# Norm factors and row sums through DRAM on GpSimd's queue, a doubled sample column in the second norm, and low parts on 128 columns

## The chip, the cores and the metric

The kernel runs on one core of a Trainium2 chip. Such a core has five engines with instruction streams of their own: TensorE (PE in the profile; its weight loads are listed apart as PEld) multiplies matrices, VectorE (DVE) and ScalarE (ACT) work elementwise and reduce along rows, GpSimd (POOL) does the same more slowly, and SyncE (SP) issues nearly all transfers (DMAs) between DRAM and the on-chip memory. Engines wait for each other and for transfers through semaphores. Metric: device time of one execution in microseconds; less is better.

## The reference

One inference step of a two-layer decoder on 256 prompt tokens and 64 sample tokens (8 sequences of 8), all in float32, with 1024 model columns. Layer A is a spatial-gating MLP, layer B an mLSTM; each is followed by a gated MLP with a short convolution. What the change touches:

```python
def rmsnorm(x, g):
    y = x * rsqrt(mean(x * x, axis=-1) + EPS)       # one factor per token
    return y * g

def chunk_spatial_gating(x, w_in, ln_g, ln_b, w_s, b_s, w_out):   # layer A, x already rmsnormed
    h = gelu(x @ w_in)
    u, v = split(h, 2, axis=-1)                      # 2048 columns each
    v = layernorm(v) * ln_g + ln_b
    ws = where(tril, w_s, 0)                         # 8 groups of 128 x 128
    mixed = einsum('gts,bnsgd->bntgd', ws, v) + b_s  # tokens mixed in chunks of 128
    return (u * mixed) @ w_out, v
```

Two vectors matter here. The norm factor of a token scales everything that is computed from it. The row sum of ws (over s, for each group g and token t) is needed because ln_b, the same for all tokens, goes through the mixing as ln_b times the row sum.

## The kernel before

Activations are kept transposed: 1024 model columns as 8 blocks k of 128 partitions, the 320 tokens along the free axis (256 prompt, then 64 sample). Weights come from DRAM as float32 chunks `raw` of 128 x 1024 on SP's queue, several ahead. Each chunk is split for TensorE into a high part `wh` (a cast to the rounded type fp32r, on ScalarE, line 180) and a low part `wl = raw - wh` (VectorE, line 181). Activations are split in the same way into xh and xl. A product is three matmuls: xh by wh, xl by wh, xh by wl. All matmuls are issued through one helper, line 49.

The norm factor isn't applied to the activations before the product but to its result. Squares of x are summed over blocks into `acc` (128 x 320). `norm_cols` turns it into factors by token on partitions (`rc`, 128 x 3: two groups of 128 prompt tokens and one of tokens 192 to 319, of which the last 64 are the samples): three matmuls by a matrix of ones into `pc`, a scale on VectorE, a power on GpSimd. `norm_row` needs the same factors along the free axis, on all partitions (`rb`, 128 x 320): it splits rc, multiplies it into an identity (`dg`), and two matmuls `pb` with ones as the stationary side spread the diagonals over all partitions; ScalarE copies them to `rb`.

Layer A (`layer_a`) first computes v with tokens on partitions. The 2048 columns of v are done in four groups q of 512, each over the 8 blocks k; for each k the two prompt groups take three matmuls each into `pv`, and the sample group two into `pvs`: the stationary side xs holds the 64 sample columns of xh on its left and those of xl on its right, and gives high times wh and low times wh at once on 128 partitions; the product of the high samples by wl needs only the left 64 columns, and uses only those. Results of group q are taken (gelu) while the next group runs. Between the groups stand small steps:

- after four blocks of q=1, norm_cols;
- after q=1, `load_ws`: loads of the mixing matrix `ws_a` (512 KB), a block copy `wss_a` for the samples, masks `trit` and `bdt`, the bias `bs_a` and the gate weights `wg`, and their masking on GpSimd;
- after q=2, `norm_row` and `row_sums`, which splits ws_a into high and low parts and adds its rows by four matmuls with ones (`pr`), copied to `rs_a` on ScalarE.

Then comes u with tokens on the free axis, column block by column block, scaled by rb. Before the mixing, VectorE adds ln_b times rs_a and bs_a into `b`.

Layer B (`layer_b`) uses the norms anew: norm_cols and norm_row are called inside its first products, and `norm_twice` beside them. It doubles the 64 sample columns of acc in another arrangement of the tokens and gets factors `rc2` for them by one more matmul. Layer B's sample products use an xs of 256 columns: one half for wh, one (high samples and zeros) for wl. The last projection (`pyt`) again uses 64 columns for its low parts.

The order of instructions on an engine is that in which a scheduling framework places the calls; it can place an instruction ahead of others that the code calls earlier. Each engine runs its stream in order, and an instruction whose input isn't there holds all behind it on that engine.

Of the kernel before, what the change touches and what calls it, by code (L numbers as in the profile page):

```python
# [39 lines left out]
class Net:  # L40
# [215 lines left out]
    def norm_cols(self, parts=None):  # L256

        nc = self.nc
        parts = parts or [self.acc]
        pc = self.psa.tile([P, 512], F32, tag="pa", name="pc")  # L260
        pv = pc[:, 0:6].rearrange("p (t e) -> p t e", e=2)
        for t in range(3):
            for i, a in enumerate(parts):
                self.mm(pv[:, t, :], self.tokens(a, t), self.ones[:, :2], i == 0, i == len(parts) - 1)
# [6 lines left out]
    def norm_twice(self):  # L271

        nc = self.nc
        acc2 = self.tp.tile([P, P], F32, tag="acc2", name="acc2", bufs=1)
        nc.scalar.copy(self.spread(acc2), self.twice(self.acc[:, TP:]))
        pc = self.psa.tile([P, 512], F32, tag="pa", name="pc2")
        self.mm(pc[:, 0:2], acc2, self.ones[:, :2], True, True)
        ms = self.tp.tile([P, 1], F32, tag="ms2", name="ms2", bufs=1)
        rc = self.tp.tile([P, 1], F32, tag="rc2", name="rc2", bufs=1)
        nc.vector.tensor_scalar(ms, pc[:, 0:1], 1.0 / D, EPS, op0=MULT, op1=ADD)  # L280
        nc.gpsimd.tensor_tensor(rc, ms, self.mhalf, op=ALU.pow)
        self.rc2 = rc

    def norm_row(self):
# [6 lines left out]
        for half in range(2):  # L291
# [3 lines left out]
            nc.vector.tensor_scalar(dg[:, half, TP:], self.ident[:, 64:], rc[:, half, 2:3], None, op0=MULT)  # L295
# [52 lines left out]
    def residual_norm(self, m, ps, gcol):  # L348
# [22 lines left out]
    def layer_a(self):  # L371
        nc, tc, I, O = self.nc, self.tc, self.I, self.O
        with tc.tile_pool(name="ya", bufs=1) as yp, tc.tile_pool(name="la", bufs=1) as lp:
# [8 lines left out]
            rsum = lp.tile([P, NH, P], F32, name="rs_a")  # L382
            trit = lp.tile([P, P], F32, name="trit")
# [4 lines left out]
            def load_ws():  # L388
                nc.sync.dma_start(ws, I["a_ws"])
                nc.sync.dma_start(trit, I["trit"])  # L390
# [1105 lines left out]
```

## Time and profile before

| What | us |
|---|---|
| median of 3 runs (lowest and highest) | 941.3 (940.94 to 941.33) |
| the profiled execution | 940.76 |
| its span in the trace | 939.0 |
| TensorE busy | 932.2 (99% of the span) |
| VectorE busy | 685.1 (73%) |
| ScalarE busy | 510.3 (54%) |
| GpSimd busy | 106.1 (11%) |
| 16 DMA engines, all queues | about 54% of the span, 167 GB/s |

Rows of the timeline below read: start in us, duration in us, engine, line, operation, output <- inputs, sizes, and in brackets how long the engine was idle before and what ended it. Rows of groups read: line, engine, operation, output <- inputs, size, count, then busy time in us and mean of one in ns, then idle time before. A row of a line or a tile alone has the shortest, median and longest duration in ns. Rows of transfers read: output <- input, queue, count, KB each, and the median of us from issue to landing; in a timeline, their duration is that of the issue. Matmul durations overlap, since they are pipelined. A row of a stretch gives the busy time of each engine with its number of instructions, then TensorE's granted clock, the busy share of the DMA engines, and GB/s.

### The profile page before, as it was taken

To read this page: it belongs to the slowest core of one execution; us is meant where nothing else is said; L and a number is where in the kernel's file an instruction comes from. 1 tells how busy PE (TensorE), PEld (TensorE's weight loads), DVE (VectorE), ACT (ScalarE), POOL (GpSimd) and SP (SyncE) were. 2 spreads that over 40 slices of the span, in tenths; PEclk is the share of its full clock that TensorE was granted. 3 is DMA by queue.
4 is the path that set the end of the run, shared out by engine and by line. 5 is a ranking of instruction groups with operands and counts; after the bars stand their busy time and mean duration, and the time that the engine had idled before them with its cause. 6 is when DMAs were issued, how large, how long until landed. Compare 5 with 4: busy or idle time off the path is not lost.

```text
span 939.0 us, 16786 instructions
## 1 busy us (share of the span) xinstructions
PE 932.2 (99%) x6345; PEld 900.4 (96%) x6345; DVE 685.1 (73%) x1258; ACT 510.3 (54%) x897; POOL 106.1 (11%) x316
## 2 busy tenths in 40 slices
PE   9999999999999999999999999999999999999997
PEld 8789999999999999998989989989999999999997
DVE  6767985597777764458999988787689777775541
ACT  7568544355455444347777776475646545544332
POOL 2200000011000001113321101000002110100001
PEclk9999999999999999999999999999999999999999
DMA  8656444445545545556675747645474545545621
GB/s 290 213 147 174 139 142 155 143 152 153 144 153 154 141 151 151 151 169 225 197 248 176 231 156 240 213 146 165 148 216 152 149 148 153 150 141 154 204 81 57
DMA packets 59330, 156.61 MB, mean 167 GB/s; under 512 B 8033, under 2 KB 21097, under 8 KB 59249
## 3 DMA queue, kind: packets, MB, share of 16 engines
q1 hardware_dynamic: 59104, 155.28, 53.6%
q8 instruction: 50, 0.82, 0.4%
q14 instruction: 32, 0.25, 0.1%
q10 hardware_dynamic: 144, 0.26, 0.1%
HBM read 143.56 MB, written 11.95 MB: 166 GB/s over the span
## 4 chain that ended last, share of the span: by engine, by line
PE 97%; DVE 2%; POOL 0%; issue 0%; ACT 0%; POOLq 0%; DVEq 0%; ACTq 0%
PE pm L49 76%; PE pv L49 9%; PE pvs L49 3%; PE num L49 2%; PE pyt L49 1%; PE pmix L49 1%; PE py L49 1%; PE pCp L49 1%; PE pcs L49 1%; PE psc L49 0%; PE pw L49 0%; PE phn L52 0%; DVE bcv L911 0%; DVE wl L181 0%; PE pk L52 0%
## 5 line engine op out<-in xcount | busy, mean ns | idle before, releaser
L180 ACT CAST wh<-raw 128x1024 fp32r<-128x1024 f32 (+4 forms) x252 | 254.9, 1012 | 283.9 <-PE pm L49 154.1
L181 DVE TENSOR_TENSOR wl<-raw,wh 128x1024 fp32r<-128x1024 f32 (+4 forms) x252 | 298.4, 1185 | 118.4 <-ACT wh L180 115.3
L49 PE MATMUL pm<-xh,wh 128*128 128x320 f32 x1088 | 338.5, 311 | 0.0
L49 PE MATMUL pm<-xh,wl 128*128 128x320 f32 x1088 | 336.2, 309 | 0.0
L49 PE MATMUL pm<-xl,wh 128*128 128x320 f32 x1088 | 336.1, 309 | 0.0
L49 PEld LDWEIGHTS pm<-xh,wh 128*128 128x128 f32 x1088 | 204.3, 188 | 1.7 <-ACT wh L180 0.5
L49 PEld LDWEIGHTS pm<-xl,wh 128*128 128x128 f32 x1088 | 204.3, 188 | 0.2
L49 PEld LDWEIGHTS pm<-xh,wl 128*128 128x128 f32 x1088 | 204.2, 188 | 0.0
L49 PE MATMUL pm<-yh_f,wh 128*128 128x320 f32 x308 | 95.2, 309 | 0.0
L49 PE MATMUL pm<-yl_f,wh 128*128 128x320 f32 x308 | 94.9, 308 | 0.0
L49 PE MATMUL pm<-yh_f,wl 128*128 128x320 f32 x308 | 94.9, 308 | 0.0
L49 PEld LDWEIGHTS pm<-yl_f,wh 128*128 128x128 f32 x308 | 57.8, 188 | 0.0
L49 PEld LDWEIGHTS pm<-yh_f,wh 128*128 128x128 f32 x308 | 57.8, 188 | 0.0
L49 PEld LDWEIGHTS pm<-yh_f,wl 128*128 128x128 f32 x308 | 57.7, 187 | 0.0
L598 DVE SCALAR_TENSOR_TENSOR fcv<-fpad,vecs,fcv 128x336 f32<-128x336 f32 x88 | 49.8, 566 | 1.5
L49 PE MATMUL pv<-wh,xh 128*128 128x512 f32 (+1 forms) x132 | 50.5, 388 | 0.0
L49 PE MATMUL pv<-wh,xl 128*128 128x512 f32 (+1 forms) x132 | 50.3, 386 | 0.0
L49 PE MATMUL pv<-wl,xh 128*128 128x512 f32 (+1 forms) x132 | 50.1, 385 | 0.0
L346 DVE TENSOR_TENSOR xT<-pm,xT 128x320 f32<-128x320 f32 x38 | 18.6, 491 | 32.3 <-PE pm L49 32.3
L49 PE MATMUL pm<-yhb,wh 128*128 128x320 f32 x128 | 39.9, 312 | 0.0
L49 PE MATMUL pm<-yh_a,wh 128*128 128x320 f32 x128 | 39.7, 310 | 0.0
L49 PE MATMUL pm<-yl_a,wh 128*128 128x320 f32 x128 | 39.6, 309 | 0.0
(340 smaller groups left out, 1458.2 us busy)
## 6 DMA issues: line engine op xcount, KB each, us to landing
raw<-in_f_up SPq DMA_DIRECT2D x88, 512.0 KB, 3.6
raw<-in_b_win SPq DMA_DIRECT2D x32, 512.0 KB, 3.8
raw<-in_f_dn SPq DMA_DIRECT2D x28, 448.0 KB, 3.4
C<-in_C SPq DMA_DIRECT2D x32, 258.0 KB, 5.6
raw<-in_a_win SPq DMA_DIRECT2D x16, 512.0 KB, 3.7
raw<-in_a_wo SPq DMA_DIRECT2D x16, 512.0 KB, 3.7
raw<-in_b_wv SPq DMA_DIRECT2D x16, 512.0 KB, 3.5
out_Cs<-C SPq DMA_DIRECT2D x32, 256.0 KB, 4.9
```

Of the source, the lines that this page charges most:

```text
L49: self.pin(self.nc.tensor.matmul(out, lhsT, rhs, start=start, stop=stop))
L180: self.last_split = nc.scalar.copy(wh[:, c, :], raw[:, c, :])
L181: self.last_low = nc.vector.tensor_tensor(wl[:, c, :], raw[:, c, :], wh[:, c, :].bitcast(F32), op=SUB)
L346: self.nc.vector.tensor_tensor(x, ps[:, :T], x, op=ADD)
L598: nc.vector.scalar_tensor_tensor(cv, pd[:, i:i + NC], self.vec(w + i * KF), cv, op0=MULT, op1=ADD)
```

## The change

- Layer A, norm row: `norm_row` isn't called. rc is written to a row of DRAM (`sums`) on GpSimd's queue as soon as it is there.
- Layer A, row sums: a second copy of the mixing matrix with t on partitions (`wn_a`, 512 KB) is loaded on SP's queue behind ws_a, masked to its lower triangle on GpSimd, and reduced on VectorE to 128 x 8 (`rs8_a`, which the program's names show as rs_a). That is written to the same row of DRAM, and the row (1408 floats) is read back onto all 128 partitions (`back_a`, 720 KB), both on GpSimd's queue. ScalarE copies rb and rs_a out of it. pb, pr and the split of ws_a go.
- Layer B: ScalarE's doubled sample columns of acc (`acc2`) are made earlier and are the input of norm_cols' third matmul; norm_twice, its matmul, scale and power go. norm_row there multiplies the third column of factors into a loaded matrix `pick` (32 KB) in the place of the identity's right half.
- Low parts of samples (wl) use all 128 columns of xs, in layer A, in layer B and in the last projection; layer B's xs has 128 columns and its memset goes.

```diff
 
-    def norm_cols(self, parts=None):
+    def norm_cols(self, side=None):
 
         nc = self.nc
-        parts = parts or [self.acc]
         pc = self.psa.tile([P, 512], F32, tag="pa", name="pc")
...
         for t in range(3):
-            for i, a in enumerate(parts):
-                self.mm(pv[:, t, :], self.tokens(a, t), self.ones[:, :2], i == 0, i == len(parts) - 1)
+            a = side if side is not None and t == 2 else self.tokens(self.acc, t)
+            self.mm(pv[:, t, :], a, self.ones[:, :2], True, True)
         rc = self.tp.tile([P, 3], F32, tag="rc", name="rc", bufs=2)
...
 
-    def norm_twice(self):
+    def twofold(self):
 
-        nc = self.nc
         acc2 = self.tp.tile([P, P], F32, tag="acc2", name="acc2", bufs=1)
-        nc.scalar.copy(self.spread(acc2), self.twice(self.acc[:, TP:]))
-        pc = self.psa.tile([P, 512], F32, tag="pa", name="pc2")
-        self.mm(pc[:, 0:2], acc2, self.ones[:, :2], True, True)
-        ms = self.tp.tile([P, 1], F32, tag="ms2", name="ms2", bufs=1)
-        rc = self.tp.tile([P, 1], F32, tag="rc2", name="rc2", bufs=1)
-        nc.vector.tensor_scalar(ms, pc[:, 0:1], 1.0 / D, EPS, op0=MULT, op1=ADD)
-        nc.gpsimd.tensor_tensor(rc, ms, self.mhalf, op=ALU.pow)
-        self.rc2 = rc
+        self.nc.scalar.copy(self.spread(acc2), self.twice(self.acc[:, TP:]))
+        return acc2
+
+    def norm_back(self, rows):
+
+        nc = self.nc
+        rows = rows.rearrange("p (c t) -> p t c", t=3)
+        self.rb = self.tp.tile([P, T], F32, tag="rb", name="rb", bufs=1)
+        nc.scalar.copy(self.rb[:, :TP].rearrange("p (t c) -> p t c", c=P), rows[:, :2, :])
+        nc.scalar.copy(self.rb[:, TP:], rows[:, 2, 64:])
 
...
                 rc[:, half, :2].unsqueeze(2).to_broadcast([P, 2, P]), op=MULT)
-            nc.vector.tensor_scalar(dg[:, half, TP:], self.ident[:, 64:], rc[:, half, 2:3], None, op0=MULT)
+            nc.vector.tensor_scalar(dg[:, half, TP:], self.pick, rc[:, half, 2:3], None, op0=MULT)
         pb = self.psa.tile([P, 512], F32, tag="pa", name="pb")
...
         if gcol == V_MIX + 8:
-            rows = self.xs[:, m, :].rearrange("p (j g d s) -> p j d g s", j=2, g=4, d=2)
+            rows = self.xs[:, m, :].rearrange("p (g d s) -> p d g s", g=4, d=2)
             xh, xl = [x[:, m, TP:].rearrange("p (g s) -> p g s", g=4) for x in (self.xh, self.xl)]
-            self.nc.gpsimd.tensor_copy(rows[:, :, 0], xh.unsqueeze(1).to_broadcast([P, 2, 4, 16]))
-            self.nc.gpsimd.tensor_copy(rows[:, 0, 1], xl)
+            self.nc.gpsimd.tensor_copy(rows[:, 0], xh)
+            self.nc.gpsimd.tensor_copy(rows[:, 1], xl)
 
...
             rsum = lp.tile([P, NH, P], F32, name="rs_a")
+            wn = lp.tile([P, NH, P], F32, name="wn_a")
+            rs8 = lp.tile([P, NH], F32, name="rs8_a")
             trit = lp.tile([P, P], F32, name="trit")
...
                 nc.sync.dma_start(ws, I["a_ws"])
+                nc.sync.dma_start(wn, I["a_wsn"])
                 nc.sync.dma_start(trit, I["trit"])
...
             def row_sums():
-                wh = self.wsp.tile([P, 8, P], F32R, tag="wh", name="wh")
-                wl = self.wsp.tile([P, 8, P], F32R, tag="wl", name="wl")
-                self.split(wh, wl, ws)
-                one = self.ones.bitcast(F32R)
-                for i in range(2):
-                    pr = self.psa.tile([P, 512], F32, tag="pa", name="pr")
-                    for j, w in enumerate((wh, wl)):
-                        self.mm(pr, one, w[:, 4 * i:4 * i + 4, :], j == 0, j == 1)
-                    nc.scalar.copy(rsum[:, 4 * i:4 * i + 4, :].rearrange("p g t -> p (g t)"), pr)
+                nc.gpsimd.affine_select(wn, wn, pattern=[[0, NH], [-1, P]], compare_op=ALU.is_ge, fill=0.0, base=0, channel_multiplier=1)
+                nc.vector.tensor_reduce(rs8, wn, axis=mybir.AxisListType.X, op=ADD)
+                nc.gpsimd.dma_start(I["sums"][:, 3 * P:].rearrange("o (t g) -> t (o g)", g=NH), rs8)
+
+            def sums_back():
+                back = lp.tile([P, 11 * P], F32, name="back_a")
+                nc.gpsimd.dma_start(back, I["sums"].to_broadcast([P, 11 * P]))
+                self.norm_back(back[:, :3 * P])
+                nc.scalar.copy(rsum, back[:, 3 * P:].rearrange("p (t g) -> p g t", g=NH))
 
...
                     self.mm(pv[2][:, c], xs, wh[:, c], k == i == 0, False)
-                    self.mm(pv[2][:64, c], xs[:, :64], wl[:, c], False, False)
+                    self.mm(pv[2][:, c], xs, wl[:, c], False, False)
 
...
                     self.mm(pv[t], xh, wl, False, k == KD - 1)
-                if k == 0:
-                    self.mm(pv[2], xs, wh, True, False)
-                self.mm(pv[2][:64], xs[:, :64], wl, False, False)
-                if k > 0:
-                    self.mm(pv[2], xs, wh, False, k == KD - 1)
+                self.mm(pv[2], xs, wh, k == 0, False)
+                self.mm(pv[2], xs, wl, False, k == KD - 1)
 
...
                         self.norm_cols()
+                        nc.gpsimd.dma_start(I["sums"][:, :3 * P].rearrange("o (c t) -> c (o t)", t=3), self.rc)
                         v_gelu(0, waiting)
...
                 if q == 2:
-                    self.norm_row()
                     row_sums()
+                if q == 3:
+                    sums_back()
                 if q in (1, 3):
...
                 xs = yh[:, k, TP:TP + P]
-                self.mm(a[:64], xs[:, :64], wl, False, False)
-                self.mm(a, xs, wh, False, last)
+                self.mm(a, xs, wh, False, False)
+                self.mm(a, xs, wl, False, last)
 
...
             mxb = lp.tile([P, 64], F32, name="mxb")
+            self.pick = lp.tile([P, 64], F32, name="pick")
             gm = lp.tile([P, 4, NH], F32, name="gm")
...
                 RS2 = rp.tile([P, P], F32, name="RS2")
+                acc2 = self.twofold()
+                nc.sync.dma_start(self.pick, I["pick"])
                 nc.sync.dma_start(bif, I["b_if"])
...
                 self.rows(p0, wh, wl, 5, self.x_rhs, True, False)
-                self.norm_cols()
+                self.norm_cols(acc2)
                 self.rows(p0, wh[:, 5:, :], wl[:, 5:, :], 3, lambda k: self.x_rhs(5 + k), False, True)
...
                 self.norm_row()
-                self.norm_twice()
                 self.rows(p1, wh[:, 5:, :], wl[:, 5:, :], 3, lambda k: self.x_rhs(5 + k), False, True)
...
                     k = kn * c + i
-                    mm(pv[2], self.xs[:, k, :P], wh[:, i, :], k == 0, False)
-                    mm(pv[2], self.xs[:, k, P:], wl[:, i, :], False, k == KD - 1)
+                    mm(pv[2], self.xs[:, k, :], wh[:, i, :], k == 0, False)
+                    mm(pv[2], self.xs[:, k, :], wl[:, i, :], False, k == KD - 1)
 
...
                     src = (vs if t == 2 else pv[t]).rearrange("p (e v) -> p e v", e=2)
-                    sc = self.rc[:, t:t + 1] if t < 2 else self.rc2
+                    sc = self.rc[:, t:t + 1] if t < 2 else self.rc[:, 2:]
                     hi, lo = vh[:, t, :, :DV], vl[:, t, :, :DV]
...
             self.xl = xp.tile([P, KD, T], F32R, name="xl")
-            self.xs = xp.tile([P, KD, 2 * P], F32R, name="xs")
-            nc.gpsimd.memset(self.xs.bitcast(F32), 0.0)
+            self.xs = xp.tile([P, KD, P], F32R, name="xs")
             self.vecs = cp.tile([P, NVEC], F32, name="vecs")
...
     a["a_ws"] = np.ascontiguousarray(ws.transpose(2, 0, 1))
+    a["a_wsn"] = np.ascontiguousarray(ws.transpose(1, 0, 2))
     a["a_wss"] = np.ascontiguousarray(np.tile(ws[:, :NS, :NS].transpose(2, 0, 1), (NB, 1, NB)))
...
         [low, (1 - odd) * sign, odd * sign, (1 - odd) * low, odd * low, sign], axis=1)], axis=1).astype(f)
+    a["pick"] = ((tok[:, None] == q[None, :]) & (low[:, None] == 0)).astype(f)
     a["mxb"] = np.where((tok[:, None] // NS == q[None, :] // NS) & (tok[:, None] <= q[None, :]), f(-1e30), f(1e4))
...
     O = {k: nc.dram_tensor("out_" + k, s, F32, kind="ExternalOutput").ap() for k, s in _OUTS.items()}
-    I["rows"] = nc.dram_tensor("rows", (8, 456), F32, kind="Internal").ap()
+    for k, v in dict(rows=(8, 456), sums=(1, 11 * P)).items():
+        I[k] = nc.dram_tensor(k, v, F32, kind="Internal").ap()
     with tile.TileContext(nc) as tc:
```

In GpSimd's stream the two writes and the read-back stand between the maskings (DMA is the issue of a transfer). Before:

```order
L268 TENSOR_TENSOR rc<-ms,mhalf 128x3
L398 TENSOR_TENSOR ws_a<-ws_a,trit 128x1024
L400 TENSOR_TENSOR wss_a<-wss_a,bdt 64x8x64 x2
L397 TENSOR_TENSOR wg<-wg,xT 128x256
L497 TENSOR_TENSOR rstd_a<-ve_a,mhalf 128x3
```

After:

```order
L473 DMA sums<-rc 128x3
L406 AFFINE_SELECT wn_a<-wn_a 128x1024
L401 TENSOR_TENSOR ws_a<-ws_a,trit 128x1024
L403 TENSOR_TENSOR wss_a<-wss_a,bdt 64x8x64
L408 DMA sums<-rs_a 128x8
L403 TENSOR_TENSOR wss_a<-wss_a,bdt 64x8x64
L412 DMA back_a<-sums 128x1408
L400 TENSOR_TENSOR wg<-wg,xT 128x256
L499 TENSOR_TENSOR rstd_a<-ve_a,mhalf 128x3
```

The read-back of `sums` is issued behind all but one of the maskings, and the write ahead of it behind two of them and the reduction.

In ScalarE's stream, at the end of q=2 in layer A (the casts of `raw` are those of the weight chunks, v_a and vs the taking of group results):

```order
 L455 ACTIVATE v_a<-vs,rc 64x512
-L180 CAST wh<-raw 128x1024 x2
-L359 CAST wh<-ws_a 128x1024
+L180 CAST wh<-raw 128x1024
+L281 COPY rb<-back_a 128x256
+L282 COPY rb<-back_a 128x64
+L414 COPY rs_a<-back_a 128x1024
+L180 CAST wh<-raw 128x1024 x2
 L453 ACTIVATE v_a<-pv,rc 128x512 x2
-L180 CAST wh<-raw 128x1024
-L300 COPY rb<-pb 128x320
-L411 COPY rs_a<-pr 128x512 x2
```

The code calls sums_back behind the products of q=3, but the copies out of back_a are placed ahead of the cast of q=3's first chunk; before, the copies out of pb and pr stood behind it.

In TensorE's stream, at the same seam, before:

```order
L49 MATMUL pvs<-wl,xh 64x512
L49 MATMUL pvs<-wh,xh 128x512
L49 MATMUL pb<-dg,ones 128x320 x2
L49 MATMUL pr<-wh,ones 128x512
L49 MATMUL pr<-wl,ones 128x512
L49 MATMUL pr<-wh,ones 128x512
L49 MATMUL pr<-wl,ones 128x512
L49 MATMUL pv<-wh,xh 128x512
L49 MATMUL pv<-wh,xl 128x512
```

After:

```order
L49 MATMUL pv<-wl,xh 128x512
L49 MATMUL pvs<-wh,xh 128x512
L49 MATMUL pvs<-wl,xh 128x512
L49 MATMUL pv<-wh,xh 128x512
L49 MATMUL pv<-wh,xl 128x512
L49 MATMUL pv<-wl,xh 128x512
```

Between the last matmul of q=2 (pvs) and the first of q=3 (pv) nothing is left.

More of the change, by code (lines that the diff above doesn't have):

```diff
@@ L269, in norm_cols @@
         self.rc = rc
-    def norm_twice(self):
-        nc = self.nc
-        acc2 = self.tp.tile([P, P], F32, tag="acc2", name="acc2", bufs=1)
-        nc.scalar.copy(self.spread(acc2), self.twice(self.acc[:, TP:]))
-        pc = self.psa.tile([P, 512], F32, tag="pa", name="pc2")
-        self.mm(pc[:, 0:2], acc2, self.ones[:, :2], True, True)
-        ms = self.tp.tile([P, 1], F32, tag="ms2", name="ms2", bufs=1)
-        rc = self.tp.tile([P, 1], F32, tag="rc2", name="rc2", bufs=1)
-        nc.vector.tensor_scalar(ms, pc[:, 0:1], 1.0 / D, EPS, op0=MULT, op1=ADD)
-        nc.gpsimd.tensor_tensor(rc, ms, self.mhalf, op=ALU.pow)
-        self.rc2 = rc
+    def twofold(self):
+        acc2 = self.tp.tile([P, P], F32, tag="acc2", name="acc2", bufs=1)
+        self.nc.scalar.copy(self.spread(acc2), self.twice(self.acc[:, TP:]))
+        return acc2
+    def norm_back(self, rows):
+        nc = self.nc
+        rows = rows.rearrange("p (c t) -> p t c", t=3)
+        self.rb = self.tp.tile([P, T], F32, tag="rb", name="rb", bufs=1)
+        nc.scalar.copy(self.rb[:, :TP].rearrange("p (t c) -> p t c", c=P), rows[:, :2, :])
+        nc.scalar.copy(self.rb[:, TP:], rows[:, 2, 64:])
     def norm_row(self):
```

## The prediction

> **What bounds the kernel.** I read the head of the profile page and its chain of waits first, then what TensorE waits for, then the timeline of each engine around the three places that the diff touches, and last the transfers.
>
> ```profile
> span 939.0 us, 16786 instructions
> PE 97%; DVE 2%; POOL 0%; issue 0%; ACT 0%; POOLq 0%; DVEq 0%; ACTq 0%
> PE pw L49 <- PEq L1477: 0.8, 1, 0.8
> ```
>
> TensorE holds 97% of the chain that ends last, and the third line is the whole list of its waits: 0.8 us, once, before the first matmul. So the time is the length of TensorE's own stream. A matmul taken out is worth the distance to the next start, not its busy time (durations overlap), and a microsecond by which weights come too late is a microsecond of the total.
>
> Place one is the seam in layer A between column groups q=2 and q=3:
>
> ```profile
> 49.56 0.40 PE L49 MATMUL pvs<-wh,xh 128*128 128x512 f32 x1
> 49.80 0.46 PE L49 MATMUL pb<-dg,ones 128*128 128x320 f32 x2
> 50.09 0.39 PE L49 MATMUL pr<-wh,ones 128*128 128x512 f32 x1
> ...
> 50.79 0.40 PE L49 MATMUL pr<-wl,ones 128*128 128x512 f32 x1
> 51.02 0.40 PE L49 MATMUL pv<-wh,xh 128*128 128x512 f32 x1
> ```
>
> Group q=2 ends with the first row; the norm row (pb) and the row sums (pr) follow; q=3 begins with the last row. Place two is the second norm, in layer B:
>
> ```profile
> 427.74 0.46 PE L49 MATMUL pb<-dg,ones 128*128 128x320 f32 x2
> 428.04 0.28 PE L49 MATMUL pc<-ones,acc 128*128 128x2 f32 x2
> 428.18 0.39 PE L49 MATMUL pm<-xh,wh 128*128 128x320 f32 x1
> 428.41 0.31 PE L49 MATMUL pm<-xl,wh 128*128 128x320 f32 x1
> 428.55 0.31 PE L49 MATMUL pm<-xh,wl 128*128 128x320 f32 x1
> ```
>
> **What it removes.** Layer A: pb and the four pr are gone, so q=3 may begin at 49.80 instead of 51.02: 1.22 us. Layer B: norm_twice's pc is gone. The next pm moves from 428.18 to 428.04, and its own pitch falls from 0.23 us behind the small matmul to the usual 0.14 (428.41 to 428.55): 0.14 + 0.09 = 0.23 us.
>
> Low parts on 128 columns, in the column groups of layer A and in the last projection:
>
> ```profile
> L49 PE MATMUL pvs<-wl,xh 128*64 128x512 f32 x30 | 11.9, 397 | 0.0
> L49 PE MATMUL pvs<-wh,xh 128*128 128x512 f32 x30 | 11.7, 389 | 0.0
> L49 PE MATMUL pyt<-wl,yh_f 128*64 128x256 f32 x12 | 2.8, 278 | 0.0
> L49 PE MATMUL pyt<-wl,yh_f 128*128 128x256 f32 x12 | 3.3, 279 | 0.0
> ```
>
> The moving side sets a matmul's length, so doubling the columns of the stationary side costs nothing: 397 ns with 64 columns against 389 with 128, and 278 against 279. The ends are nothing gained and 30 × 8 ns = 0.24 us; I take 0.24 for the first pair, as the 8 ns lie between rows of the same tile, and 0 for the second; a loss is excluded, since the wider rows are not the longer ones where they matter. Sum of what leaves TensorE: 1.22 + 0.23 + 0.24 = **1.69 us**.
>
> **Moved work with no price.** VectorE and ScalarE lose the building of dg and the split of ws_a in layer A, GpSimd a memset at the start; none was on the chain. The doubled column of acc is still copied by ScalarE, now for the third matmul of norm_cols:
>
> ```profile
> 423.14 0.30 ACT L275 COPY acc<-acc 128x128 f32<-128x128 f32 x1 [0.92 <-DVE acc L241]
> 423.55 0.72 PE L49 MATMUL pc<-ones,acc 128*128 128x2 f32 x6
> ```
>
> It ends at 423.44, before the group starts; if it came later, TensorE would wait by that much. The 32 KB load of pick stands on SP's queue ahead of bst and its followers and pushes each by about one issue (0.4 us), long before their use. The first use of rb on VectorE (ur, 70.1 us) is 20 us behind this place.
>
> **What it adds: a new chain, and a wait on ScalarE.** The sums now go: load of wn on SP, masking on GpSimd, reduction on VectorE, write to DRAM, broadcast of 720 KB back, both transfers on GpSimd's queue behind the masking of ws_a and wss_a. ScalarE takes the broadcast into rb and rs_a *ahead of* the cast (wh) that the first matmul of q=3 needs:
>
> ```profile
> 40.16 1.05 ACT L180 CAST wh<-raw 128x1024 fp32r<-128x1024 f32 x1
> 42.70 1.05 ACT L180 CAST wh<-raw 128x1024 fp32r<-128x1024 f32 x1 [1.49 <-issue]
> 51.05 0.43 ACT L300 COPY rb<-pb 128x320 f32<-128x320 f32 x1
> 51.36 1.08 ACT L411 COPY rs_a<-pr 128x512 f32<-128x512 f32 x2
> 43.78 1.23 DVE L181 TENSOR_TENSOR wl<-raw,wh 128x1024 fp32r<-128x1024 f32 x1 [1.16 <-ACT wh L180]
> ```
>
> The cast at 42.70 is that of q=3's first chunk; until now it had 7 us to spare. After the change it stands behind three copies that wait for the broadcast, and all later casts stand behind it; VectorE's wl waits for wh and stands behind the two additions of rs_a. Call T the moment the broadcast has landed. The copies take from 51.05 to 52.44 = 1.39 us by the old rows (as many elements and instructions as now); cast and wl, from 42.70 to 45.01, take 2.31. So wl is there at T + 3.70. The third matmul of q=3 needs it two pitches behind 49.80, at 50.26 (51.02 to 51.26 was one, 0.23). **TensorE waits as soon as T is past 46.56, by T − 46.56.**
>
> Now T. The rows:
>
> ```profile
> 26.45 0.42 SPq L390 DMA_DIRECT2D trit<-in_trit  x1
> ws_a<-in_a_ws SPq DMA_DIRECT2D x1, 512.0 KB, 5.1
> bs_a<-in_a_bs SPq DMA_DIRECT2D x1, 512.0 KB, 5.1
> raw<-in_a_wv SPq DMA_DIRECT2D x7, 512.0 KB, 4.2
> bdt<-in_bdt SPq DMA_DIRECT2D x2, 16.0 KB, 4.1
> bB<-in_a_ln_b SPq DMA_DIRECT2D x2, 128.0 KB, 6.8
> 30.18 2.41 POOL L398 TENSOR_TENSOR ws_a<-ws_a,trit 128x1024 f32<-128x1024 f32 x1 [1.20 <-DMA trit<-in_trit]
> 32.67 2.96 POOL L400 TENSOR_TENSOR wss_a<-wss_a,bdt 64x512 f32<-64x512 f32 x2
> L1017 POOL TENSOR_SCALAR_AFFINE_SELECT w<-w x16: 287/292/1020, 450.7 to 620.4; 128x128 f32<-128x128 f32 x16
> 44.00:50.00 6.00, 6.00 (x28) 4.75 (x28) 2.66 (x3) 2.21 (x3) 0.00 (x0) 1.00 0.90 231
> 445.36 0.26 SPq L871 DMA_DIRECT2D rows<-RS  x1
> 447.16 5.47 SPq L1067 DMA_DIRECT2D mb<-rows  x3
> 34.41 2.89 DVE L181 TENSOR_TENSOR wl<-raw,wh 128x1024 fp32r<-128x1024 f32 x1
> ```
>
> Step by step, with both ends:
> - wn (512 KB) is issued where trit stood, 26.45, and lands like ws_a: 5.1 (4.2 as the raws do) → 31.55.
> - Mask of 1024 columns: 287 ns for 128 columns is 2.3 us if all of it scales and about 1.0 if some 0.18 us of it is start-up; I take 1.2 → 32.75.
> - ws_a 2.41 → 35.16; first wss_a half of 2.96, 1.48 → 36.64. The reduction on VectorE lies beside these.
> - Write of rs8 (4 KB) until it may be read: 1.8 us between the quiet pair of rows at 445.36 and 447.16; a 16 KB load in this busy stretch took 4.1. I take 3.0 → 39.64. The second wss_a half hides in it.
> - The broadcast back: bs_a, also a broadcast, took 5.1 for 512 KB; 208 KB more at the 231 GB/s of this stretch are 0.9: 6.0. The ends are 3.1 (720 KB at that rate alone) and 6.8 + 2.6 = 9.4 (bB, and 592 KB more at that rate).
> - No transfer of before is issued by GpSimd in this stretch, so what its issue costs has no row; SP's took 0.3 to 0.6 each. I take 0.6 twice, 1.2.
>
> (In the row from 44.00 the last two numbers are the busy share of the DMA engines and GB/s, the 1.00 ahead of them the granted clock.) T = 39.64 + 6.0 + 1.2 = **46.8**, and the wait is 46.8 − 46.56 = **0.3 us**. With all low ends T is 30.65 + 1.0 + 2.41 + 1.48 + 1.8 + 3.1 = 40.4: no wait. With all high ends 31.55 + 2.3 + 3.89 + 4.1 + 9.4 + 1.2 = 52.4: a wait of 5.8 us. A gain beyond 1.69 is excluded: nothing else leaves TensorE.
>
> **A rule weighed.** Row first: a 512 KB broadcast on SP's queue took 5.1 us. The Trainium skill, page "DMA: Bandwidth & Descriptors", section "Anatomy of one DMA — SWDGE (gpsimd) path", fits a GpSimd-issued transfer as about 2.0 us plus its bytes over 436 GB/s. As an estimate by that page the write takes 2.0 and the broadcast 3.7, T is 42.3, and there is no wait; no run here shows it yet, and the fit is of transfers without the neighbours that keep this stretch's DMA engines 0.90 busy.
>
> **The sum.** 1.69 − 0.3 = 1.4 us less. The profiled execution took 940.76 (span 939.0 and 1.76 around it), which is 0.54 under the median of 941.3; from the execution I get 939.4, and against the median **939.9**.
>
> **Rivals.** *The broadcast is early enough (T under 46.56).* For it: every step of T was taken above its low end, and 0.3 us less anywhere is enough. Against: the DMA engines are 0.90 busy from 44 us on, and GpSimd's issue has no row. Time: 941.3 − 1.69 = 939.6.
>
> *The broadcast is late, and the kernel slower.* One mechanism: T past 50.1, when the wait is 3.6 us, outweighs the 1.69 and leaves 1.9 us of loss. Place: ScalarE's copies ahead of q=3's first cast. For it: T needs only 3.3 us more than my sum, and a write of 4.1 with a broadcast of 8.2 does it; a transfer as small as bB took 6.8 here; and where GpSimd's masks and VectorE's splits ran together, 1.66 us were lost (wl at 34.41 took 2.89 against 1.23), on VectorE's side now, on GpSimd's if the turn falls the other way. Against: two steps have to be near their high ends at once. At the far end, T = 52.4, the time is 939.6 + 5.8 = 945.4; a middle value, T = 51, gives 944.0.
> The Trainium skill, page "SBUF — State Buffer", section "Who interferes with whom", says that GpSimd can be kept from writing its descriptors while VectorE holds the shared ports in a two-port mode, but counts tensor_tensor, which is what VectorE runs here, as taking only the read side of that pair; by that rule VectorE's splits would not delay the two transfers, and the collision above is one of reads.
>
> *The change does not shorten TensorE* (the freed slots are filled by a wait for weights as such): for it, the margin of the cast was 7 us of ScalarE time; against it, that same 7 us. It stays under "late".
>
> **How the numbers follow.** About 0.2% of 941.3, 1.9 us, is what a measurement of this kernel can tell from no change: 939.4 and 943.2. Chances: a short wait (T from 46.56 to 50.1, times 939.6 to 943.2) 0.47, the likeliest; no wait, 939.6, 0.36; late 0.17. No wait falls on either side of 939.4 if the 0.24 of the columns or the medians are off by 0.2; I give a third of it, 0.12, to faster. So faster 0.12, same 0.71, slower 0.17. The range runs from 939.2 (no wait, medians off by 0.4) to 943.6 (T = 50.5); it leaves out about 0.05 below and 0.14 above.
>
> **What would show it.** Right: pb and pr gone behind q=2's last pvs, pv of q=3 starting 0.23 us behind it or waiting for ACT wh under 1 us; the broadcast landing around 46 to 48; pm following pb in layer B at the 0.15 pitch; no row 128*64 with 512 columns. Wrong: TensorE's waits listing ACT wh or DVE wl at q=3 with several microseconds, a broadcast landing past 50, or a granted clock under 1.00 in the slices from 44 to 60 us (it is 1.00 in the row above). A wait at any other place (norm_cols in layer B on the copy of acc, a raw load pushed by wn) is outside my sum.

## The result, and the profile after

The change made the kernel slower: median 946.14 us (944.14 to 947.34, 6 runs) against 941.12 (940.86 to 941.51, 6 runs), a ratio of 1.0052 with a 95% interval of 1.0042 to 1.0061, or 5.0 us. The profiled execution of the changed kernel is the fastest of its six: 944.14 us, span 942.3, granted clock 0.999. The other five took 945.45 to 947.34, with clocks of 0.995 to 0.997. So there are two losses to find: 3.4 us between the two profiled executions, and some 2 us more in most runs.

TensorE's list of waits in the changed kernel, which had held one entry, and then each engine's share of the chain that ended last, in which ScalarE and the transfers now have 1% each:

```profile
PE pv L49 <- ACT wh L180: 3.6, 2, 2.8
PE pw L49 <- PEq L1482: 0.8, 1, 0.8
PE pv L49 <- DVE wl L181: 0.5, 1, 0.5
```

```profile
PE 96%; DVE 2%; ACT 1%; issue 1%; DMA 1%; POOL 0%; SPq 0%; POOLq 0%; DVEq 0%; ACTq 0%
```

The two wh waits are 2.8 us at q=3 and 0.8 us at 9 us, in the start-up; the wl wait is at q=3 too. TensorE at the seam, changed kernel:

```profile
49.92 0.39 PE L49 MATMUL pvs<-wl,xh 128*128 128x512 f32 x1
53.08 0.50 PE L49 MATMUL pv<-wh,xh 128*128 128x512 f32 x1 [2.77 <-ACT wh L180]
53.42 0.39 PE L49 MATMUL pv<-wh,xl 128*128 128x512 f32 x1
54.34 0.50 PE L49 MATMUL pv<-wl,xh 128*128 128x512 f32 x1 [0.53 <-DVE wl L181]
```

pb and pr are gone, as they should be, but q=3 doesn't begin at 50.15; it begins at 53.08. ScalarE shows why:

```profile
39.29 1.05 ACT L180 CAST wh<-raw 128x1024 fp32r<-128x1024 f32 x1 [0.58 <-PE pvs L49]
49.45 0.53 ACT L281 COPY rb<-back_a 128x256 f32<-128x256 f32 x1 [9.11 <-DMA back_a<-sums]
49.88 0.27 ACT L282 COPY rb<-back_a 128x64 f32<-128x64 f32 x1
50.06 2.02 ACT L414 COPY rs_a<-back_a 128x1024 f32<-128x1024 f32 x1
51.99 1.99 ACT L180 CAST wh<-raw 128x1024 fp32r<-128x1024 f32 x2
```

It stood idle for 9.11 us for the read-back, with q=3's casts queued behind, then spent 2.54 us on the three copies. The way to that landing, on GpSimd and in the transfers:

```profile
32.74 1.09 POOL L406 TENSOR_SCALAR_AFFINE_SELECT wn_a<-wn_a 128x1024 f32<-128x1024 f32 x1 [2.07 <-DMA wn_a<-in_a_wsn]
33.81 3.37 POOL L401 TENSOR_TENSOR ws_a<-ws_a,trit 128x1024 f32<-128x1024 f32 x1
38.50 0.59 POOL L408 DMA_DIRECT2D sums<-rs_a  x1
41.04 0.59 POOL L412 DMA_DIRECT2D back_a<-sums  x1 [0.24 <-issue]
```

```profile
sums<-rs_a POOLq DMA_DIRECT2D x1, 4.0 KB, 2.0
back_a<-sums POOLq DMA_DIRECT2D x1, 704.0 KB, 8.4
```

(The profile's KB are 1024 bytes. Its 704 KB are the 720 of the prediction, where the 208 KB more than bs_a should have been 192; that is under 0.1 us.)

Where the 3.3 us between the spans (939.0 and 942.3) came from is read from the starts of the same matmuls in both traces: norm_cols of layer A, the first of u, the first of the last projection, and the last of all. First before, then after:

```profile
27.10 0.72 PE L49 MATMUL pc<-ones,acc 128*128 128x2 f32 x6
65.71 0.31 PE L49 MATMUL pm<-xh,wh 128*128 128x320 f32 x1
871.07 0.38 PE L52 MATMUL pyt<-ident,xT 128*128 128x128 f32 x2
932.88 0.28 PE L49 MATMUL pyt<-wl,yh_f 128*128 128x256 f32 x1
```

```profile
27.70 0.50 PE L49 MATMUL pc<-ones,acc 128*128 128x2 f32 x4
68.53 0.30 PE L49 MATMUL pm<-xh,wh 128*128 128x320 f32 x1
873.81 0.38 PE L52 MATMUL pyt<-ident,xT 128*128 128x128 f32 x2
936.14 0.27 PE L49 MATMUL pyt<-wl,yh_f 128*128 128x256 f32 x1
```

Start +0.60; the stretch with the seam +2.22 (40.83 against 38.61); all up to the last projection −0.08; the last projection +0.52 (62.33 against 61.81). Together 3.26. Two of the kernels below split the seam's 2.22. In late nothing waits at the seam; noseam has pb and pr as before and, in this stretch, only the wider low parts of the change. The two starts in late, then in noseam (whose helper stands one line lower):

```profile
28.04 0.28 PE L49 MATMUL pc<-ones,acc 128*128 128x2 f32 x2
64.99 0.30 PE L49 MATMUL pm<-xh,wh 128*128 128x320 f32 x1
```

```profile
28.18 0.17 PE L50 MATMUL pc<-ones,acc 128*128 128x2 f32 x1
66.37 0.30 PE L50 MATMUL pm<-xh,wh 128*128 128x320 f32 x1
```

36.95 and 38.19 us, against 38.61 before. So the low parts, with their new order, save 0.42; the missing pb and pr save 1.24; and the waits cost 3.88 (40.83 against 36.95). In the trace above the waits are 2.93 at the first matmul of q=3 (53.08 against 50.15) and 0.69 at its third, and behind each of them the next matmul comes after 0.34 us and not 0.23.

### The profile page after: what moved, and what is told of

Read it like the earlier page. It is cut to its first block, busy times and chain, and to the rows that moved or that the text cites. A ratio compares the mean times of both kernels' runs of the same rounds, so it can differ in the third digit from the quotient of the medians.

```text
span 942.3 us, 16774 instructions
## 1 busy us (share of the span) xinstructions
PE 931.3 (99%) x6337; PEld 900.7 (96%) x6337; DVE 681.0 (72%) x1252; ACT 510.0 (54%) x895; POOL 106.9 (11%) x318
## 4 chain that ended last, share of the span: by engine, by line
PE 96%; DVE 2%; ACT 1%; issue 1%; DMA 1%; POOL 0%; SPq 0%; POOLq 0%; DVEq 0%; ACTq 0%
PE pm L49 76%; PE pv L49 9%; PE pvs L49 3%; PE num L49 2%; PE pyt L49 1%; PE pmix L49 1%; PE py L49 1%; PE pCp L49 1%; DMA raw<-in_a_wv 1%; PE pcs L49 1%; PE psc L49 0%; DVE wl L181 0%; PE phn L52 0%; DVE bcv L915 0%; PE pk L52 0%
## 5 line engine op out<-in xcount | busy, mean ns | idle before, releaser
L49 PE MATMUL pm<-yhb,wl 128*128 128x320 f32 x128 | 39.5, 309 | 0.0
```

Of the source, the lines that this page charges most:

```text
L49: self.pin(self.nc.tensor.matmul(out, lhsT, rhs, start=start, stop=stop))
```

## The experiments

Times in us; the interval is that of the ratio to the kernel before in the same runs.

| kernel | median (range, runs) | ratio, 95% |
|---|---|---|
| changed | 946.14 (944.14–947.34, 6) | 1.0052 [1.0042, 1.0061] |
| late | 940.27 (939.74–941.32, 11) | 0.9989 [0.9981, 0.9998] |
| fill | 945.84 (942.97–947.04, 6) | 1.0044 [1.0031, 1.0057] |
| stall16 | 943.86 (942.89–945.42, 9) | 1.0027 [1.0017, 1.0036] |
| stall18 | 947.38 (946.46–948.14, 5) | 1.0063 [1.0051, 1.0075] |
| stall20 | 948.50 (948.23–949.39, 5) | 1.0077 [1.0065, 1.0089] |
| stall18fill | 945.12 (944.65–946.51, 5) | 1.0041 [1.0029, 1.0054] |
| actback | 941.25 (940.26–943.02, 11) | 1.0000 [0.9991, 1.0009] |
| spback | 939.77 (939.63–940.85, 11) | 0.9986 [0.9977, 0.9994] |
| noseam | 941.38 (940.71–943.12, 11) | 1.0003 [0.9994, 1.0012] |
| noseampad | 941.18 (940.67–941.61, 11) | 1.0001 [0.9992, 1.0010] |
| late64 | 939.82 (939.17–940.32, 11) | 0.9983 [0.9974, 0.9992] |
| late64pad | 939.85 (939.43–940.38, 11) | 0.9987 [0.9978, 0.9995] |
| late64mem | 939.75 (939.25–940.34, 11) | 0.9985 [0.9976, 0.9994] |
| sp64 | 939.95 (939.54–940.49, 11) | 0.9986 [0.9978, 0.9995] |

**late: is the place of the copies the loss?**

```diff
-                self.norm_back(back[:, :3 * P])
-                nc.scalar.copy(rsum, ...)
+                with tc.issue_after(self.last_split.ins):   # behind all casts of q=3 and one of u
+                    self.norm_back(back[:, :3 * P])
+                    nc.scalar.copy(rsum, ...)
```

> The changed kernel, with one difference: ScalarE's three copies out of back_a stand behind all four casts of q=3 and the first of u's weights, so that no cast waits for the read-back. Theory (the wait of the casts is the loss, with what hangs on it): TensorE shows no wait at q=3, u begins about 3.8 us earlier than in the changed kernel, and the time is near 940.0, from 939.4 (if nothing else was lost) to 940.6 (if the later start in the first 12 us and the longer last projection belong to the change). The granted clock is 0.999 in each run. Rival (the extra 1.2 MB of transfers and the software queue hold the weights up wherever the copies stand): waits for raw or wh stay, the time is above 942.

940.27, inside what the first theory gave, and TensorE runs from q=2 into q=3 without a gap:

```profile
50.26 0.39 PE L49 MATMUL pvs<-wl,xh 128*128 128x512 f32 x1
50.49 0.39 PE L49 MATMUL pv<-wh,xh 128*128 128x512 f32 x1
```

The read-back was no quicker in that trace (8.9 us to landing). The trace is that of the slowest of its eleven runs and has two waits at other places: 0.8 us for wh in the start-up, and 0.2 us of layer B's pb for dg. So the 5.9 us between this and the changed kernel hang on what stood behind the wait in ScalarE's stream, and not on the transfer's being slow as such.

**fill, stall18, stall20, stall16, stall18fill: the other 2 us.** First, matmuls in the wait of the changed kernel (cut: the lines that set up pf and xf):

```diff
                 if q == 2:
                     row_sums()
...
+                    for i in range(13):
+                        self.mm(pf, self.ones.bitcast(F32R), xf, i == 0, i == 12)   # result unused
```

> The changed kernel with 13 extra matmuls of 512 columns (ones by xl, result unused) on TensorE between q=2 and q=3, about 2.95 us, that is in the wait for the read-back. Theory C (the idle TensorE loses its clock in most runs, and this is the 2 us by which the median of the changed kernel, 946.1, exceeds its profiled run, 944.1): with TensorE busy the clock stays 0.999 in each run and the median falls to 944.0 to 944.6, although TensorE does 3 us more. Theory J (the landing of the read-back scatters, and the profiled run was a lucky one): the median stays at 945.5 to 946.5 and the runs scatter by over 2 us as before. Theory E (the matmuls count as any others): 949.

945.84: the number of theory J, but the trace doesn't speak for it. The read-back took 9.9 us this time, so that TensorE still idled 1.6 and 0.5 us, and its clock fell all the same (the third number from the right is the granted clock, ahead of the DMA share and GB/s):

```profile
52.00:55.00 3.00, 1.29 (x5) 0.42 (x3) 1.47 (x3) 3.00 (x4) 0.00 (x0) 1.00 0.00 0
55.00:58.00 3.00, 2.57 (x7) 2.04 (x8) 2.97 (x5) 2.85 (x5) 0.00 (x0) 0.63 0.53 142
```

The six runs part by their mean clock: three at 0.997 took 946.82 to 947.04, three at 0.998 or 0.999 took 942.97 to 944.86. That fits a TensorE that loses its clock when idle, but fill was to keep it busy, and did so only in part: a wait that scatters is a bad place for this test. The next kernels make the wait without any transfer, on top of late (cut: the scratch tile junk, and the arguments of the copy):

```diff
+            d = None
+            if i == 12:                       # first chunk of q=3
...
+                    for _ in range(18):       # 16, 20
+                        d = nc.scalar.copy(junk, ...)
...
-                self.last_split = nc.scalar.copy(wh[:, c, :], raw[:, c, :])
+                with self.tc.issue_after(d.ins) if d else ExitStack():
+                    self.last_split = nc.scalar.copy(wh[:, c, :], raw[:, c, :])
```

> As late, with 18 copies of 128x512 on ScalarE (to a scratch tile) ahead of q=3's first cast: a wait of TensorE of some 3.4 us for wh and 0.8 for wl that does not hang on any transfer. Theory C (an idle TensorE loses its clock): late plus 4, and about 2 more in most runs, in which the clock is 0.995 to 0.997: some 945 to 947. Theory J (only the read-back's landing scatters): late plus 4, 943.5 to 944.5, with a scatter under 0.7 us and a clock of 0.999.

> As stall18 with 20 such copies: TensorE waits some 5.2 us for wh and 0.8 for wl. Theory C: late plus 6, and 2 to 4 more in every run, clock under 0.998 in each: 947 to 950. Theory J: late plus 6, 945.5 to 946.5, clock 0.999.

The waits of TensorE in stall18, in stall20, and windows of 3 us of stall18:

```profile
PE pv L49 <- ACT wh L187: 4.1, 1, 4.1
```

```profile
PE pv L49 <- ACT wh L187: 6.1, 1, 6.1
```

```profile
46.00:49.00 3.00, 3.00 (x15) 2.48 (x14) 0.00 (x0) 2.87 (x6) 0.00 (x0) 1.00 0.92 238
49.00:52.00 3.00, 0.41 (x2) 0.00 (x0) 1.39 (x2) 2.95 (x7) 0.00 (x0) 0.97 0.05 17
52.00:55.00 3.00, 1.44 (x3) 0.72 (x4) 2.20 (x3) 2.97 (x5) 0.00 (x0) 0.50 0.00 0
55.00:58.00 3.00, 3.00 (x8) 2.32 (x9) 2.77 (x3) 1.20 (x2) 0.00 (x0) 0.50 0.75 198
58.00:61.00 3.00, 3.00 (x13) 2.46 (x12) 0.08 (x1) 1.05 (x1) 0.00 (x0) 0.90 0.82 272
```

Behind the idle time the clock is at half: eight matmuls fit into a window that otherwise holds fifteen. stall18 is 7.1 us above late for a wait of 4.1, stall20 8.2 above it for one of 6.1, so 3.0 and 2.1 us come on top, and the longer wait does not add more than the shorter. That is theory C; theory J had 944 and 946. The Trainium skill, page "TensorE: Matmul & The Clock Gate", section "What's actually happening", lets the clock drop to half after at least one idle window of about 3.4 us and come back after as long a busy one. This trace agrees with the half clock (0.50) and with its length of a few microseconds; but the clock was below 1.00 here before 52 us, less than 3 us into the wait, and fill's fall behind waits of 1.6 and 0.5 us shows that no unbroken 3.4 us are needed.

The cross-check keeps the wait of stall18 and gives TensorE 21 unused matmuls in it:

> As stall18 (ScalarE's 18 copies ahead of q=3's first cast, TensorE idle for 4.1 us, 947.4), with 21 unused matmuls of 512 columns (4.8 us) on TensorE between q=2 and q=3, so that it is not idle there. Theory C (the idle time lowers TensorE's clock, and the half clock behind it costs some 2 us beside the wait): the clock stays 1.00 from 52 to 61 us, 0.999 in the mean, and the time falls by about 2 us, to 945.0 to 945.8, though TensorE has 21 matmuls more. Rival (the slow matmuls behind the wait come from something else in those microseconds, transfers or ScalarE): they stay slow and the time is 948 or more.

```profile
52.00:55.00 3.00, 3.00 (x14) 2.22 (x12) 1.81 (x2) 2.98 (x5) 0.00 (x0) 1.00 0.00 0
55.00:58.00 3.00, 2.96 (x14) 2.36 (x13) 2.94 (x4) 1.60 (x2) 0.00 (x0) 1.00 0.63 168
```

The window from 49 reads like the one from 52, the clock stays at 1.00, and the time falls from 947.38 to 945.12, which is late and the 4.8 us of the unused matmuls, with more work on TensorE. The half clock is shown to come from the idle time.

> As stall18 with 16 copies: TensorE idle for about 1.3 us for wh and 0.8 for wl at q=3. Theory C with a threshold of some 3 us of idle time: the clock stays 0.999 and the time is late plus the wait, 942.2 to 942.6. Theory C without a threshold near there (the clock is judged by the share of busy time in a stretch, as fill's fall behind 1.6 + 0.5 us of idle time suggests): it falls in some runs, which are then 1.5 us longer, and the runs scatter between 942.3 and 944.

943.86, with runs from 942.89 to 945.42. The profiled run (943.03, waits of 1.8 and 0.5 us) has a clock of 0.999 and lies 2.8 above late. The nine runs part by their mean clock: four at 0.999 took 942.89 to 943.15, five at 0.997 took 943.86 to 945.42. So the clock falls in some runs even behind such waits, as in fill; where it fell in these five is not shown, as they have no trace. In the changed kernel it is the same: its traced run waited 2.8 and 0.5 and kept its clock, while the other five show means of 0.995 to 0.997. The nearest trace of a fall there is that of contig (below), the changed kernel with a shorter copy: 946.51 us, mean clock 0.996, a wait of 3.1 us at q=3, and then:

```profile
52.00:55.00 3.00, 1.70 (x3) 0.99 (x4) 2.38 (x4) 3.00 (x5) 0.00 (x0) 0.53 0.00 0
55.00:58.00 3.00, 3.00 (x8) 2.35 (x8) 2.94 (x5) 2.37 (x4) 0.00 (x0) 0.50 0.78 208
```

From norm_cols to u it takes 43.20 us, 2.4 more than the changed kernel's own trace (40.83), though it waits no longer. So the half clock at the seam, and not only a lower mean, is seen there too.

**spback and actback: why the read-back was late.**

```diff
-                nc.gpsimd.dma_start(back, I["sums"].to_broadcast([P, 11 * P]))
+                nc.sync.dma_start(back, ...)      # spback;  actback: nc.scalar
```

> The changed kernel with the read-back of 704 KB issued on SP's queue in the place of GpSimd's; by this ScalarE's copies stand behind the first two casts of q=3. Theory Q (the software queue makes the read-back slow): it lands within 6.0 to 6.6 us of its issue, as I had estimated from broadcasts on SP's queue. Theory S (its size and its neighbours make it slow): 8 to 10 us, as in the changed kernel (8.4). The time is 940 to 941 in both, since no cast waits for it, unless SP's queue, which now waits for the writes, brings the raws of u too late: then TensorE shows waits behind q=3.

> The changed kernel with the read-back issued on ScalarE's queue, a hardware queue apart from SP's, so that SP's own order stays that of the changed kernel; the copies stand ahead of q=3's first cast as there. Theory Q (GpSimd's software queue is what makes the read-back slow): it lands 6.0 to 6.6 us after its issue, near 47, TensorE waits 1 to 2 us at q=3, and the time is 941 to 942.5. Theory N (on SP's queue it was quick, 6.3 us, because the transfers behind it were held back): 8 to 10 us, landing near 50, a wait of 3 us or more and a time of 944 to 947.

spback's timeline, the issue and the first copy, which waited for the landing; then actback's transfer, and TensorE's waits in that kernel:

```profile
42.63 0.37 SPq L412 DMA_DIRECT2D back_a<-sums  x1
48.95 0.53 ACT L281 COPY rb<-back_a 128x256 f32<-128x256 f32 x1 [1.99 <-DMA back_a<-sums]
```

```profile
back_a<-sums ACTq DMA_DIRECT2D x1, 704.0 KB, 5.7
```

```profile
PE pv L49 <- ACT wh L180: 0.5, 1, 0.5
PE pv L49 <- DVE wl L181: 0.2, 1, 0.2
```

6.3 us on SP's queue (6.7 in sp64, which issues it there too) and 5.7 on ScalarE's, against 7.0 to 9.9 in eleven traces from GpSimd's queue: 7.0 in late64mem, and 8.4 or more in the others (changed 8.4, fill 9.9). That is on theory Q's side in all three, though 5.7 and 6.7 lie just outside its 6.0 to 6.6, and TensorE waits 0.7 us in actback and not 1 to 2. actback keeps SP's order and issues 1.2 us earlier than the changed kernel, so its neighbours aren't quite the same. They were no lighter, though: while the read-back ran, all queues together moved 295 to 313 GB/s in these three traces, and 205 to 282 in the eleven. That the queue makes all of the difference is not shown, that the queue makes most of it is the plain reading; late64mem's 7.0 has no explanation here. The Trainium skill, page "DMA: Bandwidth & Descriptors", section "Anatomy of one DMA — SWDGE (gpsimd) path", gave, as an estimate by its fit, 2.0 us for the write, with which the trace agrees (2.0), and 3.7 for the read-back, with which it does not: the measured 7.0 to 9.9 among busy neighbours decide. spback, at 939.77, avoids the wait as late does, since there the copies also landed behind two casts of q=3.

**contig: the copy.** `nc.scalar.copy(rsum, back[...])` in the order of back_a, not transposed.

> The changed kernel with ScalarE's copy of the row sums read in the order in which they lie (1024 neighbours) and not transposed with a step of 8; the sums stand in the wrong places, and only the time of this copy is of use. If the step of 8 makes the copy slow, it takes 1.0 to 1.1 us in the place of 2.02; if the wider copy or its source does, 2.0.

```profile
51.22 1.04 ACT L414 COPY rs_a<-back_a 128x1024 f32<-128x1024 f32 x1
```

1.04 against 2.02: the step of 8 elements doubles the copy. (Its one run took 946.51 with a clock of 0.996.)

**noseam, late64, sp64, noseampad, late64pad, late64mem, before2: the small terms.** noseam is the change without the way through DRAM and with the last projection as before; late64 is late, and sp64 is spback, with the last projection's low parts on 64 columns.

> Everything of the change but the way through DRAM: layer A builds its norm row and the row sums on TensorE as the kernel before, and the last projection keeps 64 columns. What remains are the 128 columns in layers A and B (0.24), the doubled column in norm_cols (0.23), and no memset ahead of the first products. Theory (these are worth their pitches): 941.2 less 0.47, 940.7, or 940.4 if the first q begins earlier without the memset (0.25). Rival (only the seam gives a gain): 941.2.

> As late, and the last projection's low parts are on 64 columns again, in the order of the kernel before. Theory (128 columns cost there: matmuls of 256 columns stand 120 to 124 ns apart where all have 128 columns, 117 where 64 and 128 alternate): the pitch is 117 again, the stretch of pyt 0.3 us shorter, and the time 939.9 to 940.0 against 940.27. Rival (the longer pitch belongs to the profiled execution): the pitch stays 120, the time 940.3.

> spback (read-back on SP's queue, 939.77) with the last projection's low parts on 64 columns again: 0.3 us less by its pitches, as late64 against late (0.45 in the medians): 939.3 to 939.6, faster than both. If the 0.45 was scatter: 939.8.

noseam came out at 941.38 against 941.14 in the same runs: no gain is seen, as the rival had it, though its interval just reaches the 0.47 (a ratio of 0.9995). late64 (939.82) and sp64 (939.95) cannot be told from late (940.27) and spback (939.77) by their intervals, and their traces refuted my reason: in late64's last projection the matmuls of 256 columns are still 0.12 us apart where both sides were always 128 wide. Nine starts in late64, first and last, and the same tiles before:

```profile
926.05 0.28 PE L49 MATMUL pyt<-xl,yh_f 128*128 128x256 f32 x1
...
927.01 0.28 PE L49 MATMUL pyt<-xh,yl_f 128*128 128x256 f32 x1
```

```profile
926.93 0.28 PE L49 MATMUL pyt<-xl,yh_f 128*128 128x256 f32 x1
...
927.87 0.28 PE L49 MATMUL pyt<-xh,yl_f 128*128 128x256 f32 x1
```

0.96 and 0.94 us for eight pitches, 120 and 118 ns. Over the whole last projection, from its first pyt to its last, the difference is plain: 61.81 us in both traces of the kernel before (before2 is the second), 62.21 in the six variants with 64 columns, and 62.32 or 62.33 in the changed kernel and the nine variants with 128. So the 128 columns, with their order, cost 0.12 there and not 0.3, and 0.40 has another cause. Next suspect: the smaller xs of layer B moves all tiles behind it. noseampad gives xs its old size back, late64pad half of it.

> noseam with layer B's xs allocated at its old size (256 columns for each k, half of them unused), which puts all tiles behind it back to their old places. In the last 18 us of noseam, late64 and the changed kernel alike, matmuls of 256 columns stand 119.5 to 121 ns apart, against 116 to 117 before, with 64 or 128 columns alike, so that not the columns cost there. Theory P (where the tiles lie decides it): the pitch is 116.5 again and the time 0.4 to 0.5 less than noseam's 941.38: 940.9. Rival (the changed instructions of layer B or the loads there): the pitch stays 120, the time 941.4.

> late64 with 64 unused columns for each k in layer B's xs (half of the old surplus; the whole doesn't fit beside the new tiles), so that the tiles behind it move by 2 KB in each partition. Theory P with a rule that this shift meets: the pitch of the last 18 us is 116.5 and the time 939.4; with a rule that it doesn't meet: 120 and 939.8.

The pitch stayed at 120 in both (941.18 and 939.85) and the last projection at 62.21, so this theory fell too. And the start: late64mem puts the memsets back, before2 is the kernel before once more.

> late64 with two memsets of 128x1024 on GpSimd at the start, the work that the change took from there. If the missing memset lets the first products run ahead of their weights and so costs what the first q seems to lose (0.3 us), the time is 939.5 and norm_cols begins near 27.1. If not, 939.8 to 940.1 and a start anywhere from 26.8 to 28.2.

> The kernel before once more, for a second trace of its first 30 us: in the traces of the changed kernel and of eleven variants norm_cols of layer A begins at 26.8 to 28.2 us (mean 27.5), in the one trace of before at 27.10. If the later start belongs to the change, it is again 27.0 to 27.2 here; if it is scatter of the first loads, it can be anywhere from 26.8 to 28.2. The time is 941 in both.

late64mem took 939.75, no change. before2 (941.15) begins norm_cols at 27.50 and not 27.10, so the start scatters by this much in the kernel before; the 0.60 at the start of the changed kernel's trace is of that size and is not put down to the change.

## Why the prediction was wrong, point by point

- *What bounds the kernel* and *a microsecond of late weights is a microsecond of the total*: right, but not all. Idle time of TensorE costs itself and, in most runs, some 2 us of half clock behind it. That price stood nowhere in my sum. I had listed a clock under 1.00 as something to look for, and my far end (945.4) came without it.
- *What leaves TensorE, 1.69*: the seam's 1.22 is gone from the stream, and layer B's 0.23 is there (behind pb, pm follows at the usual 0.15 in the changed kernel). The low parts were mis-sized both ways: in layer A they save 0.42 between norm_cols and u alone, since the 8 ns of a row's duration are not the change in the pitch of a block (0.42 over 20 blocks is 21 ns for each); in the last projection, where I had put 0 and excluded a loss, they cost 0.12. What the sum missed besides is the 0.40 there, which every variant shows, and some 0.15 between u and the last projection (0.08 saved where layer B alone saves 0.23). That fits noseam's zero (0.42 and 0.08 gained, 0.40 given back) and the 1.2 to 1.5 that late64, late64pad, spback, sp64 and late64mem gained.
- *Moved work with no price*: nothing there was waited for in the changed kernel.
- *The new chain, T = 46.8*: the mechanism and its place were right; this was the step that failed first, by its sizes. The read-back was issued at 41.04, 0.8 later than my sum had it: the load of wn went out at 27.12 after a late start and took 5.6, and the ws_a mask took 3.37 and not 2.41, as it began while VectorE's split ran. The write took only 2.0 and not 3.0, so that the issue waited for GpSimd's second wss_a half (to 40.79) and not for the write (40.50). The broadcast then took 8.4 where I had 6.6 with its issue, taken from SP's queue. T was 49.4.
- *The point from which TensorE waits, 46.56*: 1.15 us too late, since I priced ScalarE's copies by old ones of the same size (1.39); they took 2.54, and the strided one alone 2.02.
- The formula with the measured T and copies gives 49.4 − 46.56 + 1.15 = 4.0 us of wait against 3.6 in the trace (2.93 and 0.69); q=3 itself would have begun 0.35 us later than my 49.80.
- What each miss weighs: with the measured T alone my sum gives 942.5, still inside the range; with the measured copies 943.6, its upper end. The rest up to 946.14 is mainly the half clock, a term that I had at nothing: the trace with the full clock accounts for 2.7 of the 5.0 us lost (2.22 − 0.08 + 0.52), and the remaining 2.4 are of the size that stall18 (3.0), stall20 (2.1) and contig (2.4) show.
- *The chances*: 0.17 for the late rival was too little. It was ranked by estimates from another queue, the one row that I had said did not exist; the range should have treated it as unknown upward. That the kernel is slower needed T past 50.1 in my text; it came with T at 49.4, through the copies and the clock.

## What to carry to other kernels

Before work is moved off the bounding engine through DRAM, look at which instruction of the receiving engine takes it back, and what is queued behind it: here copies whose factors VectorE needs some 20 us later held the four casts of q=3, the first of which was needed at once. Moving the copies behind the casts (late, 0.9989; late64, 0.9983) or the transfer to SP's queue (spback, 0.9986) turns the same change from a loss of 0.5% into a gain of 0.1 to 0.2%. And price a wait of a TensorE that is otherwise never idle at more than its length: in stall18 four microseconds of it put the clock at half for some five more with matmuls running, and cost 3 us on top.

## What the runs showed of the hardware that I had not expected

- The half clock falls behind waits that are short and broken: 1.6 and 0.5 us in fill, while 2.8 and 0.5 us in the changed kernel's traced run left it at 1.00.
- 704 KB read back onto all partitions took 7.0 to 9.9 us from GpSimd's queue (eleven traces) and 5.7 to 6.7 from the queues of SP and ScalarE (three), in the same 12 us of the kernel.
- A ScalarE copy that reads every eighth element takes 2.02 us for 1024 columns, against 1.04 in order.
- A small matmul pitch adds up unseen: the order and width of the samples' low parts save 21 ns per block of layer A and cost 0.12 us in the last projection, while the mean durations of the rows differ by 8 ns and 1 ns.
- Open: the last projection takes 62.21 us or more in every variant of the changed kernel, 61.81 in both traces before. 0.12 of the changed kernel's 62.33 is the low parts; the 0.40 is neither they nor the size of xs.
